# Forgetting attention: the keys' biases as rows of the product for the maxima, and the maxima's row made by products with the identity

## The chip, the cores and the metric

One core of a Trainium2 chip runs the whole program. The metric is the device time of one execution in microseconds (us). The median of three runs of the kernel before is 1830.58 us (1828.81 to 1836.41).

## What is computed

One layer of a streaming encoder: 2,048 prompt tokens and 8 x 16 sample tokens go through an RMS norm and one wide projection, whose columns feed three mixers: forgetting attention (6 heads of 64), RWKV-7 time mixing and cross-attention to 256 memory tokens (4 heads of 64). The gated results go through an output projection. The change touches the two attentions on the prompt. Cut to what matters:

```python
def fox_attend_block(q, cq, qpos, k, v, ck, kpos):
    s = jnp.einsum('bqhd,bkhd->bhqk', q, k) * (HEAD_DIM ** -0.5)
    s = s + jnp.transpose(cq, (0, 2, 1))[..., :, None] - jnp.transpose(ck, (0, 2, 1))[..., None, :]
    s = jnp.where(kpos[None, :] <= qpos[:, None], s, jnp.finfo(jnp.float32).min)
    p = jax.nn.softmax(s, axis=-1)
    return jnp.einsum('bhqk,bkhd->bqhd', p, v)
# c = cumsum(log forget) along the tokens; memory attention is the same without c and without the mask
```

## The kernel before

The program has two parts. The first (to about 1125 us) projects the tokens and runs RWKV-7; it writes queries, keys and values to DRAM (`q_d`, `k_d`, `v_d`). At its end `forget()` (L788) sums the log forget values and writes the keys' biases, -c, as six rows of 2,048 to `nc_d`. The second part does the attentions and the output projection.

In the second part the work of forgetting attention comes in 12 **units**, one for each pair of heads `hp` (0 to 2) and block `qb` (0 to 3) of 512 queries; "unit (1,3)" is pair 1, block 3. Block `qb` sees `qb + 1` blocks of 512 keys. Memory attention has 8 units more. Around them stand the sample tokens' attention (`sample`, L1188) and the output projection (`py`).

A unit has two steps. The first, `queries` (L1034), finds for every query the largest logit. `fox_max` multiplies 128 queries by 512 keys into `pm` on TensorE (PE), and VectorE (DVE) adds the keys' biases and takes the maximum in one instruction (L1063). The biases lie in `nb`, a tile of [128, 2, 2048] into which every row of `nc_d` is copied to all 128 partitions, 256 KB in each of 24 transfers (L1011). There is one `nb`, so the next pair's biases wait until the last maximum of this pair is done. `negate` turns the signs, and `rows_` turns the eight columns of maxima into a row: a transpose on PE (`pr`), a copy on ScalarE (ACT, `m8`), a transfer to DRAM (`md`), and two transfers back into partition 64 of `Q2` (L1086, L1088).

The second step, `attend` (L1100), forms keys x queries in `pS` from two products: `K1` x `Q1` (128 rows: the keys' upper part twice, against the queries' upper and lower parts) and `K2` x `Q2` (65 rows: the keys' lower part and a row of ones, against the queries' upper part and the row of negative maxima). So the second product can't start before that row has come back. ACT takes the exponential (L1117) and its rounded copy `Ph`, GpSimd (POOL) the remainder `Pl`, and three products per tile make `po`. Two `pS` buffers and two `pm` buffers are in use.

All transfers are issued by SyncE (SP), in one order. That order, and that of every engine, is set by a planner (`_arrange`, L1881) which takes the whole program's instructions, their costs and dependences by a model, tries 15 orders, and keeps one. So an edit in the second part can change the order everywhere, the first part included.

Of the kernel before, what the change touches and what calls it, by code (L numbers as in the profile page):

```python
# [33 lines left out]
TP = 2048  # L34
# [17 lines left out]
def kernel(ctx: ExitStack, tc: tile.TileContext, I: dict, O: dict):  # L52
# [8 lines left out]
    def tt(e, out, a, b, op):  # L61
        e.tensor_tensor(out=out, in0=a, in1=b, op=op)  # L62
# [52 lines left out]
    nc_d = dt("nc_d", [6, TP])  # L115
# [7 lines left out]
    with ExitStack() as p1:  # L123
# [664 lines left out]
        def forget():  # L788
# [137 lines left out]
    with ExitStack() as p2:  # L926
# [21 lines left out]
        S.copy(negT, negm[:, 2, :])  # L948
        idb = c2t("idb", [128, 128], BF16)
# [46 lines left out]
        def fox_keys(U, hp):  # L996
# [4 lines left out]
            def block(g0):  # L1001
                if not g0:
                    U["nb"] = kp.tile([128, 2, TP], F32, tag="nb", name="nb")
                gs = slice(g0, g0 + 512)
                pt = turned_in(k_d[gs, cs], 512)
                k1 = [kp.tile([128, 512], F32R, tag="K1", name="K1", bufs=2 * NKB) for _ in range(2)]
                k2 = [kp.tile([65, 512], F32R, tag="K2", name="K2", bufs=2 * NKB) for _ in range(2)]
# [11 lines left out]
        def mem_keys(U, hp):  # L1019
            cs = slice(128 * hp, 128 * hp + 128)  # L1020

            def step():
# [3 lines left out]
                k1 = [m[:, 256 * h:256 * h + 256] for h in range(2)]  # L1026
                k2 = [m[0:65, 512 + 256 * h:768 + 256 * h] for h in range(2)]
# [6 lines left out]
        def queries(U, q, qsrc, qb, hp, fox):  # L1034

            s_ = "" if fox else "m"

            def load():
                pt = turned_in(qsrc, 512)
                if fox:  # L1040
                    q["Q1"] = [wk.tile([128, 512], F32R, tag=f"Q1{h}", name=f"Q1{h}") for h in range(2)]
                    q["Q2"] = [wk.tile([65, 512], F32R, tag=f"Q2{h}", name=f"Q2{h}") for h in range(2)]
                else:
                    m = big("Qm", F32R)
                    q["Q1"] = [m[:, 512 * h:512 * h + 512] for h in range(2)]
                    q["Q2"] = [m[0:65, 512 * h:512 * h + 512] for h in (2, 3)]
# [965 lines left out]
```

## Time and profile before

| | |
|---|---|
| median of 3 runs | 1830.58 us |
| the profiled execution: its own time | 1832.25 us |
| its span in the profile | 1830.5 us |
| PE busy | 1718.1 us, 94% of the span |
| DVE, ACT, POOL busy | 51%, 48%, 43% |
| mean clock granted to PE | 0.971 |

The profiled execution is 1.67 us slower than the median of the runs; 1.75 us of it lie around the span. PE is the busiest engine, so time is won or lost where PE is idle, or where it is granted its lower clock; both are looked for by stretches of the span. A wait in brackets, as `[5.40 <-DVE Q L62]`, is idle time of that engine just before the instruction, with what ended it. SPq rows are the issues of transfers, not the transfers themselves.

### The profile page before, as it was taken

To read this page: it belongs to the slowest core of one execution; us is meant where nothing else is said; L and a number is where in the kernel's file an instruction comes from. 1 tells how busy PE (TensorE), PEld (TensorE's weight loads), DVE (VectorE), ACT (ScalarE), POOL (GpSimd) and SP (SyncE) were. 2 spreads that over 40 slices of the span, in tenths; PEclk is the share of its full clock that TensorE was granted. 3 is DMA by queue.
4 is the path that set the end of the run, shared out by engine and by line. 5 is a ranking of instruction groups with operands and counts; after the bars stand their busy time and mean duration, and the time that the engine had idled before them with its cause. 6 is when DMAs were issued, how large, how long until landed. Compare 5 with 4: busy or idle time off the path is not lost. (4 is left out here: it accounts for less than half of the span.)

```text
span 1830.5 us, 42049 instructions
## 1 busy us (share of the span) xinstructions
PE 1718.1 (94%) x16743; PEld 1370.1 (75%) x16743; DVE 934.0 (51%) x2325; ACT 872.3 (48%) x1727; POOL 782.4 (43%) x790
## 2 busy tenths in 40 slices
PE   4989999999999999999999998799899898999998
PEld 3989989788887788887888886567576555667776
DVE  6543354474444564364754543867346654485213
ACT  5424342533243424325232433687787565986351
POOL 5565252232322243031322241377586364866562
PEclk9999999999999999999999998799999898999999
DMA  7665463644445645456454454434647645262432
GB/s 230 246 219 200 144 205 125 202 163 151 168 157 168 223 128 190 138 174 195 155 170 134 134 177 123 156 121 143 203 138 248 195 141 173 87 209 87 163 111 89
DMA packets 213273, 301.34 MB, mean 165 GB/s; under 512 B 57444, under 2 KB 162454, under 8 KB 197206
## 3 DMA queue, kind: packets, MB, share of 16 engines
q1 hardware_dynamic: 213078, 298.66, 49.6%
q8 instruction: 131, 2.15, 0.5%
q14 instruction: 64, 0.52, 0.1%
HBM read 211.47 MB, written 87.12 MB: 163 GB/s over the span
## 5 line engine op out<-in xcount | busy, mean ns | idle before, releaser
L59 PE MATMUL pjd<-xk,w 128*128 128x512 f32 (+4 forms) x2280 | 520.1, 373 | 14.6 <-DVE xk L62 6.7
L59 PEld LDWEIGHTS pjd<-xk,w 128*128 128x128 f32 (+1 forms) x2280 | 381.9, 190 | 79.1 <-issue 10.8
L62 POOL TENSOR_TENSOR Pl<-P,Ph 128x512 fp32r<-128x512 f32 (+3 forms) x272 | 315.5, 1174 | 150.5 <-ACT Ph L1120 127.6
L59 PE MATMUL pjt<-w,xk 128*128 128x256 f32 x2040 | 292.6, 291 | 4.4 <-ACT qk L705 4.4
L59 PEld LDWEIGHTS pjt<-w,xk 128*128 128x128 f32 x2040 | 263.9, 191 | 17.9 <-issue 7.7
L59 PE MATMUL py<-W,oh 128*128 128x512 f32 x816 | 236.2, 402 | 2.3 <-DVE rb L1162 1.6
L1117 ACT ACTIVATE P<-pS,NB 128x512 f32<-128x512 f32 x240 | 147.9, 623 | 85.6 <-PE pS L59 57.5
L59 PEld LDWEIGHTS py<-W,oh 128*128 128x128 f32 x816 | 150.5, 190 | 38.3 <-DVE rb L1162 2.1
L59 PE MATMUL pS<-Q,K 128*128 128x512 f32 (+2 forms) x480 | 155.5, 392 | 8.3 <-ACT P L1117 8.0
L1120 ACT CAST Ph<-P 128x512 fp32r<-128x512 f32 (+3 forms) x272 | 150.1, 564 | 7.7 <-PE po L59 2.9
L59 PE MATMUL po<-Ph,vt 128*65 128x512 f32 x480 | 151.3, 373 | 1.2 <-ACT ob L1143 0.7
L59 PEld LDWEIGHTS pS<-Q,K 128*128 128x128 f32 (+1 forms) x480 | 87.4, 195 | 40.5 <-ACT P L1117 24.7
L62 DVE TENSOR_TENSOR xo<-py,xo 128x512 f32<-128x512 f32 x68 | 46.5, 686 | 133.1 <-PE py L59 127.8
L59 PE MATMUL pm<-K,Q 128*128 128x512 f32 (+2 forms) x240 | 95.8, 411 | 19.5 <-DVE Q L62 13.1
L62 POOL TENSOR_TENSOR nr<-nr,mhalf 128x8 f32<-128x8 f32 (+2 forms) x43 | 61.2, 1424 | 122.9 <-DVE nr L68 106.4
L1063 DVE CUSTOM_DVE_ANT_0 jk<-pm,nb,mx 128x512 bf16<-128x512 f32 (+3 forms) x144 | 93.2, 647 | 33.7 <-PE pm L59 25.1
L62 POOL TENSOR_TENSOR w<-wraw,w 128x1024 fp32r<-128x1024 f32 (+1 forms) x34 | 79.6, 2343 | 46.6 <-ACT w L197 42.2
L59 PE MATMUL po<-Pl,vt 128*65 128x512 f32 x240 | 88.3, 369 | 1.8 <-POOL Pl L62 1.7
L705 ACT COPY qk<-pjt 128x512 f32<-128x512 f32 (+1 forms) x47 | 26.5, 563 | 131.0 <-PE pjt L59 104.3
L59 PEld LDWEIGHTS po<-Ph,vt 128*65 128x65 f32 x480 | 64.0, 139 | 27.3 <-ACT Ph L1120 2.4
L59 PEld LDWEIGHTS pm<-K,Q 128*128 128x128 f32 x240 | 47.1, 198 | 44.7 <-DVE mx L1063 18.2
L62 POOL TENSOR_TENSOR oh<-ot,oh 128x384 fp32r<-128x384 f32 (+2 forms) x38 | 44.9, 1183 | 74.3 <-ACT oh L1323 39.5
(392 smaller groups left out, 2820.9 us busy)
## 6 DMA issues: line engine op xcount, KB each, us to landing
w<-w_d SPq DMA_DIRECT2D x84, 1024.0 KB
w_d<-w SPq DMA_DIRECT2D x28, 1024.0 KB
y_d<-xo SPq DMA_DIRECT2D x21, 512.0 KB
wraw<-in_w_in SPq DMA_DIRECT2D x36, 256.0 KB
xo<-in_x SPq DMA_DIRECT2D x17, 512.0 KB
xo<-y_d SPq DMA_DIRECT2D x17, 512.0 KB
xt<-in_x SPq DMA_DIRECT2D x24, 256.0 KB
xraw<-in_xT SPq DMA_DIRECT2D x24, 256.0 KB
```

What stands on the lines that cost most here:

```text
L59: PE.matmul(out, lhsT, rhs, start=start, stop=stop, skip_group_check=True)
L62: e.tensor_tensor(out=out, in0=a, in1=b, op=op)
L705: S.copy(o_, out)
L1063: V.tensor_tensor_reduce(out=jk[:, :n], in0=pm[:, :n], in1=U["nb"][:, h, c0:c0 + n], scale=1.0, scalar=-3.0e38 if c0 == 0 else m_, op0=A_, ...
L1117: S.activation(P_[:, c0:], pS[:, c0:], AF.Exp, bias=NB[:, qb, 2 * hp + h, kt:kt + 1] if fox else 0.0)
L1120: S.copy(Ph[:, c0:], P_[:, c0:])
```

## The change

- `forget` writes the biases as an upper and a lower part, so `nc_d` has 12 rows; the copy out of `pn` moves to ACT, with a subtraction on DVE.
- `nb` and its 24 transfers of 256 KB go. `K1` becomes [67, 512]: the keys' upper part, a row of ones, and the two rows of the bias, which 24 transfers of 4 KB bring from `nc_d`. `Q1` becomes [67, 512]: the queries' upper part and three rows of ones, the first of which is later overwritten by the negative maximum. `K2` and `Q2` become 128 rows, and hold the two cross products.
- `fox_max` multiplies 67 rows, and its maximum is a plain reduction out of PSUM into a column of its own; a small reduction joins the columns where `qb` is not 0.
- `negate` writes columns 0 and 32 of a tile `turnm`, the rest of which is zero. `rows_` makes four products of 33 columns with the identity, and two copies on ACT of [1, 512] from PSUM straight into `Q1`. The transfers by way of `md` go, 60 in all.
- In `attend` the product without the row of maxima now comes first.

```diff
-    nc_d = dt("nc_d", [6, TP])
+    nc_d = dt("nc_d", [12, TP])
...
-            nr = sm.tile([96, 128], F32, tag="w4", name="nr", bufs=1)
-            V.tensor_copy(nr, pn[0:96, 0:128])
-            SY.dma_start(nc_d.rearrange("h (t p) -> (h t) p", p=128), nr)
+            nr = sm.tile([96, 2, 128], F32R, tag="w4", name="nr", bufs=1)
+            S.copy(nr[:, 0], pn[0:96, 0:128])
+            tt(V, nr[:, 1], pn[0:96, 0:128], nr[:, 0].bitcast(F32), SUB)
+            for a in range(2):
+                SY.dma_start(nc_d[6 * a:6 * a + 6].rearrange("h (t p) -> (h t) p", p=128), nr[:, a].bitcast(F32))
...
+        turnm = [c2t(f"turnm{j}", [128, 4, 33], F32R) for j in range(4)]
+        for x in turnm:
+            G.memset(x.bitcast(F32), 0.0)
...
         def split_keys(k1, k2, src, n):
             src = src[:, :n]
             S.copy(k1[0:64, :n], src)
-            S.copy(k1[64:128, :n], src)
-            tt(V, k2[0:64, :n], src, k1[0:64, :n].bitcast(F32), SUB)
-            G.memset(k2[64:65, :n].bitcast(F32), 1.0)
+            S.copy(k2[0:64, :n], src)
+            tt(V, k2[64:128, :n], src, k1[0:64, :n].bitcast(F32), SUB)
+            G.memset(k1[64:65, :n].bitcast(F32), 1.0)
...
                 for h in range(2):
                     split_keys(k1[h], k2[h], pt[64 * h:64 * h + 64], 512)
-                for h in range(2):
-                    SY.dma_start(U["nb"][:, h, gs], nc_d[2 * hp + h, gs].partition_broadcast(128))
+                    SY.dma_start(k1[h][65:67, :].bitcast(F32), nc_d[2 * hp + h:2 * hp + h + 7:6, gs])
...
                     S.copy(q["Q1"][h][0:64], src)
-                    S.copy(q["Q2"][h][0:64], src)
-                    tt(V, q["Q1"][h][64:128], src, q["Q1"][h][0:64].bitcast(F32), SUB)
+                    S.copy(q["Q2"][h][64:128], src)
+                    tt(V, q["Q2"][h][0:64], src, q["Q1"][h][0:64].bitcast(F32), SUB)
+                    if fox:
+                        G.memset(q["Q1"][h][64:67].bitcast(F32), 1.0)
...
-                V.tensor_tensor_reduce(out=jk[:, :n], in0=pm[:, :n], in1=U["nb"][:, h, c0:c0 + n], scale=1.0,
-                                       scalar=-3.0e38 if c0 == 0 else m_, op0=A_, op1=MAX, accum_out=m_)
+                V.tensor_reduce(out=q["mx"][:, h, t, c0 // 512:c0 // 512 + 1], in_=pm[:, :n], op=MAX, axis=AX.X)
...
             def rows_():
                 pr = qa.tile([128, 512], F32, tag="pt", bufs=PTB, name="pr")
-                PE.transpose(pr[0:8, 0:128], q["mx"].rearrange("p h t -> p (h t)"), ident)
-                m8 = wk.tile([8, 128], F32R, tag="m8", name="m8")
-                S.copy(m8, pr[0:8, 0:128])
-                md = dt("md", [8, 128], bufs=4)
-                SY.dma_start(md, m8.bitcast(F32))
+                for t in range(4):
+                    mm(pr[0:33, 128 * t:128 * t + 128], q["mr"][:, t, :], idr)
                 for h in range(2):
-                    SY.dma_start(q["Q2"][h][64:65, :].bitcast(F32), md[4 * h:4 * h + 4].rearrange("(o t) c -> o (t c)", o=1))
+                    S.copy(q["Q1"][h][64:65], pr[32 * h:32 * h + 1])
...
-                mm(pS[:, c0:], k1, q["Q1"][h][:, c0:], stop=False)
+                mm(pS[:, c0:], k2, q["Q2"][h][:, c0:], stop=False)
                 diag = fox and kt >= 4 * qb
-                mm(pS[:, c0:], k2, q["Q2"][h][:, c0:], start=False, stop=not diag)
+                mm(pS[:, c0:], k1[0:65], q["Q1"][h][0:65, c0:], start=False, stop=not diag)
```

Counted over the whole program, PE gets 80 products of 33 columns for 20 transposes; DVE loses 240 reads of an accumulator, and 240 maxima become plain reductions; ACT gets 40 copies of [1, 512] for 20 of [8, 128]; POOL gets 24 memsets of [3, 512] and 4 of [128, 132]; SP issues 1,171 transfers for 1,230. In the first part only `forget` differs in its instructions, but the planner's order there is another from its first products on.

SP at the start of the second part, where the first keys, values and queries are loaded (`tok`, `vtok`); before:

```order
L980 DMA tok<-q_d 128x4x128
L941 DMA negm<-in_negm 128x384
L1011 DMA nb<-nc_d 128x512 x6
L754 DMA mg_d<-gth 128x512
L1011 DMA nb<-nc_d 128x512
L980 DMA tok<-k_d 128x4x128
L1011 DMA nb<-nc_d 128x512
L647 DMA o_d<-bv 128x512
L754 DMA mg_d<-gth 128x512
L923 DMA out_rs_p<-sstp 64x6x64
L988 DMA vtok<-v_d 128x4x128
L980 DMA tok<-q_d 128x4x128
```

and of the change:

```order
L990 DMA tok<-q_d 128x4x128
L943 DMA negm<-in_negm 128x384
L754 DMA mg_d<-gth 128x512 x2
L925 DMA out_rs_p<-sstp 64x6x64
L647 DMA o_d<-bv 128x512
L1018 DMA K_13992<-nc_d 2x512
L990 DMA tok<-k_d 128x4x128
L998 DMA vtok<-v_d 128x4x128
L990 DMA tok<-q_d 128x4x128
L1018 DMA K_13993<-nc_d 2x512
```

Eight loads of `nb` stood ahead of the second `vtok` and `tok<-q_d`; one load of bias rows stands there now, and the other head's follows.

SP around the end of pair 1, where the biases of pair 2 are fetched; before, with the row of maxima of unit (1,3) (`md<-m`, `Q<-md`) among them:

```order
L1011 DMA nb<-nc_d 128x512
L1086 DMA md<-m_18747 8x128
L980 DMA tok<-q_d 128x4x128
L1198 DMA sC<-mg_d 128x128
L1206 DMA sC<-mq_d 128x128
L1011 DMA nb<-nc_d 128x512 x6
L1170 DMA rc<-sd 32x32
L1088 DMA Q_18194<-md 1x512
L1088 DMA Q_18195<-md 1x512
```

and of the change:

```order
L990 DMA tok<-q_d 128x4x128
L1158 DMA sd<-rs 1x512
L1210 DMA sC<-mg_d 128x128
L1218 DMA sC<-mq_d 128x128
L1018 DMA K_18810<-nc_d 2x512
L1182 DMA rc<-sd 32x32
L1018 DMA K_18811<-nc_d 2x512
L1185 DMA rd<-rc 32x32
```

The row and the six loads ahead of its return are gone from the queue.

PE from the row of maxima of unit (1,3) to that unit's first product that needs it (before `Q_18194`, the change `Q_18091`); before:

```order
L1082 MATMUL pr<-ident,mx 8x128
L59 MATMUL pS_18734<-sB,sD 32x256 x4
L1263 MATMUL pt3b<-ident,sD 128x128 x2
L59 MATMUL pS_18810<-sB,sD 32x256 x4
L1263 MATMUL pt3b<-ident,sD 128x128 x2
L59 MATMUL po_18861<-sD,sA 64x16 x32
L1211 MATMUL pt_18964<-ident,sC 128x128
L59 MATMUL pS<-Q_18194,K_16179 128x512 x2
```

and of the change:

```order
L59 MATMUL pr<-idr,turnm_13967 33x128 x4
L59 LDWEIGHTS idb
L59 MATMUL pS<-negT,idb 128x128
L59 MATMUL po<-Ph,vt 65x512
L59 MATMUL po<-Ph,vt 64x512
L59 MATMUL po<-Pl,vt 65x512
L59 MATMUL po<-Ph,vt 65x384
L59 MATMUL pS<-Q_18091,K_16117 128x512
```

Between the two stood the small products of a sample's attention (`sB`, `sD`, `sA`); now a few products of the unit before stand there.

## Rows read from the trace of the kernel before

**Rows 1.** Profile page, head and the busy time of PE.
```profile
span 1830.5 us, 42049 instructions
PE 1718.1 (94%) x16743; PEld 1370.1 (75%) x16743; DVE 934.0 (51%) x2325; ACT 872.3 (48%) x1727; POOL 782.4 (43%) x790
```

**Rows 2.** Stretches of the span: length, busy time and instructions of each engine, granted clock of PE, busy share of the DMA engines, GB/s. The first row is the first part, the last the whole second part.
```profile
0.00:1125.00 1125.00, 1071.60 (x13220) 918.40 (x13221) 554.96 (x1445) 411.34 (x859) 374.99 (x408) 0.98 0.52 172
1125.00:1170.00 45.00, 28.65 (x124) 19.06 (x122) 30.45 (x72) 23.80 (x47) 11.68 (x17) 0.62 0.66 207
1170.00:1410.00 240.00, 230.97 (x1108) 162.03 (x1109) 144.57 (x312) 185.71 (x350) 165.72 (x152) 0.99 0.49 161
1410.00:1445.00 35.00, 28.15 (x248) 17.94 (x247) 21.41 (x68) 18.82 (x41) 9.26 (x14) 0.80 0.56 182
1530.00:1550.00 20.00, 13.25 (x109) 8.39 (x107) 6.04 (x23) 8.90 (x20) 3.93 (x6) 0.66 0.84 244
1125.00:1830.50 705.50, 646.53 (x3525) 451.70 (x3523) 378.99 (x880) 460.93 (x868) 407.43 (x383) 0.95 0.47 154
```

**Rows 3.** Waits of PE in the second part (1125 to 1830): us in total, times, longest.
```profile
PE pm L59 <- DVE Q L62: 13.1, 6, 5.4
PE pS L59 <- ACT P L1117: 10.9, 12, 2.9
PE pt3b L1263 <- DVE sD L68: 8.3, 6, 3.1
PE pm L59 <- DVE mx L1063: 6.5, 13, 1.0
PE po L59 <- POOL Pl L62: 2.0, 5, 0.7
```

**Rows 4.** Start of the second part in order of time: start, us, engine, line, operation.
```profile
1127.92 4.39 SPq L1011 DMA_DIRECT2D nb<-nc_d  x6
1139.51 0.52 SPq L980 DMA_DIRECT2D tok<-q_d  x1
1151.05 0.80 PE L59 MATMUL pm<-K,Q 128*128 128x512 f32 x1 [5.40 <-DVE Q L62]
1154.69 0.87 PE L59 MATMUL pm<-K,Q 128*128 128x512 f32 x2 [2.84 <-DVE Q L62]
```

**Rows 5.** One of the stretches in it, columns as in rows 2.
```profile
1135.00:1140.00 5.00, 3.48 (x11) 2.35 (x11) 3.06 (x10) 1.53 (x4) 0.00 (x0) 0.50 1.05 366
```

**Rows 6.** Unit (1,1), from its maxima's way to DRAM to their way back, in order of time.
```profile
1417.81 0.29 SPq L1086 DMA_DIRECT2D md<-m  x1
1424.73 3.66 SPq L1202 DMA_DIRECT2D sC<-np_d  x8
1429.15 1.30 PE L1263 MATMUL pt3b<-ident,sD 128*128 128x128 f32 x5 [3.08 <-DVE sD L68]
1430.41 0.57 SPq L1088 DMA_DIRECT2D Q<-md  x2
```

**Rows 7.** Unit (1,3), the same way, to the first product that reads the row.
```profile
1532.62 0.28 SPq L1086 DMA_DIRECT2D md<-m  x1
1534.70 4.35 SPq L1011 DMA_DIRECT2D nb<-nc_d  x6
1539.57 0.57 SPq L1088 DMA_DIRECT2D Q<-md  x2
1543.10 1.22 PE L59 MATMUL pS<-Q,K 65*128 65x512 f32 x2
```

**Rows 8.** Unit (0,3) in order of time, the same way; the last row is output projection that PE took meanwhile.
```profile
1289.25 0.28 SPq L1086 DMA_DIRECT2D md<-m  x1
1294.37 0.57 SPq L1088 DMA_DIRECT2D Q<-md  x2
1300.72 4.15 PE L59 MATMUL py<-W,oh 128*128 128x512 f32 x17
```

**Rows 9.** Two stretches behind it, columns as in rows 2.
```profile
1305.00:1310.00 5.00, 3.00 (x15) 1.67 (x14) 1.29 (x2) 2.88 (x5) 2.24 (x2) 1.00 0.68 229
1310.00:1315.00 5.00, 2.23 (x6) 1.11 (x7) 2.52 (x5) 4.23 (x9) 2.61 (x3) 0.86 0.94 274
```

**Rows 10.** Groups by form, whole span: busy us, mean ns of one, then idle before.
```profile
L1063 DVE CUSTOM_DVE_ANT_0 jk<-pm,nb,mx 128x512 bf16<-128x512 f32 x90 | 67.2, 747 | 22.9 <-PE pm L59 18.4
L1063 DVE CUSTOM_DVE_ANT_0 jk<-pm,nb 128x512 bf16<-128x512 f32 x78 | 53.6, 687 | 18.4 <-PE pm L59 14.5
L1063 DVE DVE_READ_ACCUMULATOR2_ANT mx<- 128x1 f32 x240 | 19.6, 82 | 0.0
L1070 DVE TENSOR_REDUCE mx<-pm 128x2 f32<-128x512 f32 x32 | 21.3, 686 | 7.3 <-PE pm L59 7.2
L59 PE MATMUL pS<-Q,K 128*128 128x512 f32 x168 | 73.3, 438 | 6.0 <-ACT P L1117 5.7
L59 PE MATMUL pS<-Q,K 65*128 65x512 f32 x168 | 68.3, 413 | 0.0
L1139 ACT COPY rs<-po 1x512 f32<-1x512 f32 x20 | 11.6, 580 | 18.3 <-PE po L59 18.0
L975 POOL MEMSET K<- 1x512 f32 x24 | 12.1, 520 | 1.0
```

**Rows 11.** The copy of the turned maxima: duration ns min/median/max, first and last start.
```profile
L1084 ACT CAST m<-pr x20: 238/255/256, 1144.3 to 1706.2; 8x128 fp32r<-8x128 f32 x20
```

**Rows 12.** A piece of the chain that ended last: start, us, what. Four transposes of 128 columns in a row.
```profile
1308.47 0.45 PE pt L983 x4
```

**Rows 13.** A wait of SP in the second part.
```profile
SPq L1011 <- DVE mx L68: 5.5, 2, 3.5
```

More of the change, by code (lines that the diff above doesn't have):

```diff
@@ L948 @@
         S.copy(negT, negm[:, 2, :])
+        idr = c2t("idr", [128, 128], F32R)
+        S.copy(idr, ident)
+        turnm = [c2t(f"turnm{j}", [128, 4, 33], F32R) for j in range(4)]
+        for x in turnm:
+            G.memset(x.bitcast(F32), 0.0)
+        taken = [0, 0]
         idb = c2t("idb", [128, 128], BF16)
@@ L1001, in block @@
             def block(g0):
[L1002 to L1003 removed]
                 gs = slice(g0, g0 + 512)
                 pt = turned_in(k_d[gs, cs], 512)
[L1006 to L1007 removed]
+                k1 = [kp.tile([67, 512], F32R, tag="K1", name="K1", bufs=2 * NKB) for _ in range(2)]
+                k2 = [kp.tile([128, 512], F32R, tag="K2", name="K2", bufs=2 * NKB) for _ in range(2)]
                 for h in range(2):
                     split_keys(k1[h], k2[h], pt[64 * h:64 * h + 64], 512)
[L1010 to L1011 removed]
+                    SY.dma_start(k1[h][65:67, :].bitcast(F32), nc_d[2 * hp + h:2 * hp + h + 7:6, gs])
                 vt = kp.tile([128, 1032], F32R, tag="vt", name="vt", bufs=NKB)
@@ L1025, in step @@
                 pt = turned_in(mk_d[:, cs], 256)
-                k1 = [m[:, 256 * h:256 * h + 256] for h in range(2)]
-                k2 = [m[0:65, 512 + 256 * h:768 + 256 * h] for h in range(2)]
+                k1 = [m[0:65, 256 * h:256 * h + 256] for h in range(2)]
+                k2 = [m[:, 512 + 256 * h:768 + 256 * h] for h in range(2)]
                 for h in range(2):
@@ L1040, in load @@
                 if fox:
-                    q["Q1"] = [wk.tile([128, 512], F32R, tag=f"Q1{h}", name=f"Q1{h}") for h in range(2)]
-                    q["Q2"] = [wk.tile([65, 512], F32R, tag=f"Q2{h}", name=f"Q2{h}") for h in range(2)]
+                    q["Q1"] = [wk.tile([67, 512], F32R, tag=f"Q1{h}", name=f"Q1{h}") for h in range(2)]
+                    q["Q2"] = [wk.tile([128, 512], F32R, tag=f"Q2{h}", name=f"Q2{h}") for h in range(2)]
                 else:
                     m = big("Qm", F32R)
-                    q["Q1"] = [m[:, 512 * h:512 * h + 512] for h in range(2)]
-                    q["Q2"] = [m[0:65, 512 * h:512 * h + 512] for h in (2, 3)]
+                    q["Q1"] = [m[0:65, 512 * h:512 * h + 512] for h in range(2)]
+                    q["Q2"] = [m[:, 512 * h:512 * h + 512] for h in (2, 3)]
                 for h in range(2):
@@ L1068, in mem_max @@
                 for j in range(2):
[L1069 to L1070 removed]
+                    mm(pm[:, 256 * j:256 * j + 256], q["Q1"][h][0:64, 128 * (t + j):128 * (t + j) + 128],
+                       U["K1"][0][h][0:64])
+                V.tensor_reduce(out=q["mx"][:, h, t:t + 2, 0], in_=pm.rearrange("p (t k) -> p t k", k=256), op=MAX,
                                 axis=AX.X)
             def negate():
[L1074 to L1078 removed]
+                mx = q["mx"][:, :, :, 0]
+                if fox and qb:
+                    mx = wk.tile([128, 2, 4], F32, tag="m1", name="m1")
+                    V.tensor_reduce(out=mx.rearrange("p h t -> p (h t)"),
+                                    in_=q["mx"].rearrange("p h t c -> p (h t) c"), op=MAX, axis=AX.X)
+                for h in range(2):
+                    if fox:
+                        ts(V, q["mr"][:, :, 32 * h], mx[:, h], off[:, 4 * qb, 2 * hp + h:2 * hp + h + 1], -1.0, A_, M)
+                    else:
+                        ts(V, q["mr"][:, :, 32 * h], mx[:, h], -1.0, None, M, ALU.bypass)
             def rows_():
                 pr = qa.tile([128, 512], F32, tag="pt", bufs=PTB, name="pr")
[L1082 to L1086 removed]
+                for t in range(4):
+                    mm(pr[0:33, 128 * t:128 * t + 128], q["mr"][:, t, :], idr)
                 for h in range(2):
[L1088 removed]
+                    S.copy(q["Q1"][h][64:65], pr[32 * h:32 * h + 1])
             r = [load]
```

13 lines of the change are left out of this document (3 added, 10 removed).

## The prediction

> **What bounds the kernel now.** I read the page's head first: PE is busy 94% of a span of 1830.5 us [rows 1]. So no other engine's work counts by itself; what counts is where PE has nothing to do, and where it is granted its lower level. The table by stretches says where. The first part has 53.4 us without PE work in 1125 (1125 - 1071.6), spread out. Of the second part three short stretches stand out [rows 2]: its start (1125 to 1170: 16.35 us idle, granted clock 0.62), 1410 to 1445 (6.85 us idle, 0.80) and 1530 to 1550 (6.75 us idle, 0.66). A mean of 0.62 between full speed (2.4 GHz) and half (1.2 GHz) is 34 us at half; 0.80 is 14 us, 0.66 is 13.6 us. If the idle time lies in the time at half, the slower products lose half of the rest: 8.9, 3.6 and 3.4 us. So 25, 10.4 and 10.2 us can be won there at most.
>
> Then I asked the issues of transfers in each stretch what stood before PE.
> - Start: six loads of `nb` take SP 4.39 us, two more follow, and the second `tok<-q_d` is issued only at 1139.51; PE then waits 5.40 and 2.84 us for the split of those queries [rows 4]. From 1135 to 1140 the DMA engines are full (share 1.05) [rows 5].
> - Unit (1,1): the row of maxima leaves at 1417.81 and is fetched back at 1430.41, behind a sample's eight loads (3.66 us). For these 12.6 us the unit's second products can't run, and PE idles 3.08 us in a sample's chain that has nothing beside it [rows 6].
> - Unit (1,3): the row leaves at 1532.62, six `nb` loads hold SP for 4.35 us, the return is issued at 1539.57, and the first product that reads it starts at 1543.10: 10.5 us [rows 7].
> - Unit (0,3): 5.1 us between the two; PE covers it with 17 products of the output projection, and is then out of work, 4.77 us idle from 1305 to 1315 [rows 8, 9].
>
> **The change, part by part.** The sum is made against the profiled execution, 1832.25 us, 1.67 above the median of the runs.
>
> 1. *Start.* Eight loads of 256 KB go (2.1 MB; 5.7 us at the 366 GB/s of rows 5), and some 5 us of SP's issue with them; in the new order one load of bias rows stands ahead of the second `tok<-q_d`. That brings the queries forward by 4 to 6 us, and PE's two waits on them are 8.2 us. I take **-6**: most of the waits, plus some time at half clock. Bounds 0 and -12 (the waits, and nearly half of the 8.9 us of the clock). What is late next is ACT's and DVE's splitting of keys and queries, which nothing shortens.
> 2. *Unit (1,1).* The row now takes four products (four transposes of 128 columns: 0.45 us [rows 12]) and two copies of [1, 512] (0.58 each [rows 10]), 1.6 us for 12.6. In the new order the unit's own products follow within the samples' chain. **-5**, half of what is lost there; bounds 0 and -10.4. The sample's chain itself stays.
> 3. *Unit (1,3).* Here the row is all that is waited for, and both causes go. **-7**; bounds 0 and -10.2.
> 4. *Unit (0,3).* With no gap to fill, the 17 products remain for 1305 to 1315: **-2**, bounds 0 and -4.8. The other units' rows come back under dense PE work: 0.
> 5. *Maxima on DVE.* The 168 maxima of 512 columns took 67.2 + 53.6 us and 168 x 82 ns for the accumulator, 134.6 us; as plain reductions of 686 ns they take 115.2 [rows 10]. That is 19 us less on an engine off the path; what PE waits for it is 6.5 us [rows 3]. **-2**, bounds 0 and -6.5. The added small reductions and sign changes come out of that gain.
> 6. *PE.* Same number of `pm` and `pS` products and columns. 20 x 3 more small ones, 0.11 us each by rows 12, are 6.7 us if PE is dense; some fall into idle time: **+5**, bounds +2 and +6.7. `pm` has 67 rows for 128. The row of 65 rows has 413 ns, that of 128 rows 438 [rows 10]; read as a price of rows, it would be worth 168 x 25 ns = 4.2 us. I take nothing: the longer one is the first of its pair and carries the 6.0 us of waiting. The Trainium skill ("TensorE: Matmul & The Clock Gate", section "LDWEIGHTS") says that a load of 32 rows takes as long as one of 128; by it the 4.2 us are nothing too, and by the row alone the sum would be 4.2 lower.
> 7. *ACT.* 40 copies of 0.58 for 20 of 0.255 [rows 10, 11]: +18.1 us beside 460.9 busy in 705.5 [rows 2]. PE waits 10.9 us for ACT in all [rows 3]; the copies stand before a unit's first exponentials, where ACT has little to do: **+2**, bounds 0 and +18.1.
> 8. *POOL.* 24 memsets of 0.52 us [rows 10], 12.5 us beside 407 of 705.5 [rows 2]; PE waits 2.0 us for POOL [rows 3]. 0, at most +2.
> 9. *Transfers elsewhere, and the first part.* SP issues 59 fewer, and nothing waits for the rest of `nb`: 0. In the first part the instructions are the same but for `forget`; the order differs and no row says which is better: 0, within 5 either way (a tenth of its idle 53.4 us).
>
> Sum: -6 - 5 - 7 - 2 - 2 + 5 + 2 = **-15 us**, 1817.2 for the profiled execution and **1815.6** for the median of the runs (1830.58 - 15). About 0.5% (9.2 us) is what a measurement of this kernel tells from no change: below 1821.4 is faster, above 1839.7 slower.
>
> **The rivals.**
> - *The stalls move.* The row was one of several late things. For this speaks that in rows 6 the idle time just before the transposes is put down to DVE's `sD`, the sample's own chain, and that at the start ACT's splits come one after another. Against it: in rows 7 only the row was missing. And the new bias rows are a transfer too: a block's first maximum now waits for a load of 4 KB that SP can issue only when the old `K1` tile is free, with the queue behind it; SP held `nb` that way for 5.5 us already [rows 13]. Then steps 1 and 3 give 3 and 4, steps 2, 4 and 5 nothing, and with +5 and +2 the time stays at **1830.6**.
> - *ACT becomes the bound: slower.* From 1170 to 1410 ACT is busy 185.7 of 240 us [rows 2]; with 12 of the 20 units there it gets +10.9, a share of 0.82. If each copy stood ahead of an exponential that PE waits for, all 18.1 us would come on the path; steps 1 and 3 keep their 13, step 6 its 5: +10.1, **1840.7**. It decides from the point at which ACT has no idle time around a unit's start; the mean of 0.77 and the 10.9 us that PE waits for ACT now speak against it.
> - *A transfer's fixed price is all that goes.* The Trainium skill ("DMA: Bandwidth & Descriptors", section "Anatomy of one DMA") gives about 2 us for a transfer whatever its size. As a mechanism of this kernel: the row saves its two hops alone, and SP's queue stands as long as before, since other loads move up. A hop is bounded by rows 7: from its issue to the product that reads it the return takes 3.5 us, so two are 7 us of the 10.5, and of 12.6. Step 2 then shrinks to half, 2.5, and step 3 to two thirds, 4.7, and the sum to -10.2: **1820.4**. By the Trainium skill's figure, as an estimate, two hops are 4 us and the sum would be some 3 us higher still.
>
> **How the numbers follow.** Chances: the forecast 0.50, the fixed price alone 0.12, the stalls move 0.23, ACT 0.15. Faster by over 0.5%: nearly all of the forecast (0.45), more than half of the fixed price (0.08) and a third of the moved stalls, where the first part's new order may help (0.09): 0.62. Slower by over 0.5%: most of the ACT case (0.12) and a little of the moved stalls (0.02): 0.14. The rest, 0.24, is no change. All upper ends together (-12, -10.4, -10.2, -4.8, -6.5, with +2 and 0) would be -42 and 1788.7; that all come at once is unlikely, and the range stops at three quarters of it, -31.5: **1799**. Upwards it takes in the moved stalls with +3.4 for the order: **1834**. About 0.2 is left out, most of it the ACT case.
>
> **What would show it.** Right: SP's loads of keys and queries at the start issued by 1135; the three stretches gone or short, with a granted clock near 1; a unit's first product with the row 2 to 3 us behind its `pr`; DVE about 20 us less busy, ACT 18 more. Wrong: if PE idles as long at the second part's start, or the samples' chains still stand alone and at half clock, the stalls have moved; if PE's waits for ACT grow from 10.9 us by ten or more, it is ACT; if SP waits long at the loads of bias rows, it is the queue. If the first part's end moves by more than 5 us, the planner's order, which I took as neutral, decides the result.

## The result, and the profile after

The changed kernel takes 1835.79 us (median of 20 runs, 1830.02 to 1841.74), the kernel before 1831.34 beside it (20 runs): a ratio of 1.0027, 95% interval 1.0016 to 1.0037. It is slower by 0.27%, beyond the interval, but by the prediction's bound of 0.5% that is no change; it lies 20 us above the forecast and 1.8 us above the upper end of the range (1834). The head of its profile (5.1 us longer than [rows 1], with 26.6 us more PE work and 12.2 less on DVE):

```profile
span 1835.6 us, 41777 instructions
PE 1744.7 (95%) x16803; PEld 1389.7 (76%) x16803; DVE 921.8 (50%) x2102; ACT 888.8 (48%) x1749; POOL 793.3 (43%) x818
```

I divide both spans at the first transpose of the second part (`pt`, L983, now L993): 1129.68 us before, 1145.79 after. View: stretches, columns as in [rows 2]; the first 27 us, which are loads, are left out. Before:

```profile
27.00:1129.68 1102.68, 1067.99 (x13218) 915.37 (x13219) 547.49 (x1421) 401.31 (x838) 368.50 (x391) 0.98 0.52 170
1129.68:1830.50 700.82, 644.08 (x3503) 450.01 (x3502) 375.88 (x873) 459.66 (x865) 402.81 (x376) 0.95 0.47 154
```

After:

```profile
27.00:1145.79 1118.79, 1079.31 (x13222) 927.11 (x13220) 549.26 (x1418) 402.78 (x843) 369.91 (x397) 0.97 0.51 167
1145.79:1835.60 689.81, 658.38 (x3563) 458.24 (x3562) 363.11 (x650) 476.02 (x885) 414.66 (x401) 0.95 0.44 147
```

The second part became 11.0 us shorter: 25.3 us less without PE work (31.4 for 56.7), 14.3 us more PE work, with PE at half clock (1.2 GHz) for 73 us in both. The first part, in which the change touches two instructions and a DMA of `forget`, became 16.1 us longer, and 11.3 of these are PE *work*: the same products took longer.

Where it lies can be seen at the twelve RWKV chains (`gw`, `gx`: products of 32 by 32 that wait in turn for DVE and ACT). The order puts projection products (`pjd`) between their links to keep PE busy. View: timeline of one chain, before and after (start, us, engine, line, operation, idle time before it and its cause). Before:

```profile
830.71 0.75 PE L59 MATMUL gw<-x,gm 32*32 32x32 f32 x64
831.39 0.96 PE L59 MATMUL pjd<-xk,w 128*128 128x512 f32 x3
832.29 0.75 PE L59 MATMUL gw<-xd,g 32*32 32x32 f32 x64
832.97 1.90 PE L59 MATMUL pjd<-xk,w 128*128 128x512 f32 x7
834.79 0.69 PE L59 MATMUL gx<-x,gm 32*32 32x32 f32 x32
```

After:

```profile
851.27 0.75 PE L59 MATMUL gw<-x,gm 32*32 32x32 f32 x64 [0.66 <-DVE x L464]
852.49 1.05 PE L59 MATMUL gw<-xd,g 32*32 32x32 f32 x64 [0.47 <-ACT g L470]
853.47 0.45 PE L59 MATMUL pjd<-xk,w 128*70 128x512 f32 x1
855.59 1.06 PE L59 MATMUL gx<-x,gm 32*32 32x32 f32 x32 [1.67 <-DVE x L477]
```

Ten `pjd` stand between these links before, one after. The idle time of the twelve chains, each with the wait before its first link, added up from the timeline, is 7.8 us before and 17.3 after (elsewhere in the first part it falls, so that 4.8 us remain in all). It costs more than itself, since the granted clock falls behind it (stretches of the profile after):

```profile
850.00:855.00 5.00, 2.79 (x134) 2.08 (x132) 2.68 (x5) 1.91 (x5) 1.27 (x1) 0.94 0.93 311
855.00:860.00 5.00, 4.41 (x70) 2.96 (x70) 1.86 (x4) 3.39 (x8) 1.51 (x2) 0.50 0.97 340
860.00:865.00 5.00, 4.76 (x83) 3.09 (x82) 0.00 (x0) 2.34 (x5) 0.18 (x1) 0.50 0.48 157
865.00:870.00 5.00, 5.00 (x93) 4.09 (x92) 3.07 (x9) 1.11 (x4) 0.00 (x0) 0.50 0.51 200
```

Behind 2.21 us of idle time the products run at half clock (0.50) for 15 us and more. Added up over the first part, PE has half clock for 34 us before and 68 us after. The difference lies at the chains: of these times 13.7 and 47.8 us begin between the first and the last link of a chain, and 20.8 and 20.5 us elsewhere. Three chains after have only 4 to 7 projection products (`pjd`, `pjt`) between their links, where before none has fewer than 12; 30.7 of the 47.8 us begin in these three.

In the second part the waits that answer to [rows 3] (from 1145 us on: us in total, times, longest):

```profile
PE pm L59 <- DVE mx L1073: 5.0, 9, 1.2
PE pS L59 <- ACT P L1129: 4.7, 6, 2.1
PE pS L59 <- DVE Q L62: 2.6, 1, 2.6
PE pt3b L1275 <- DVE sD L68: 2.2, 2, 1.9
PE po L59 <- POOL Pl L62: 1.7, 3, 0.9
```

The longest one of before, `pm` for DVE's half of the queries (13.1 us), is gone, and those for `P` and `sD` are about half and a quarter.

### The profile page after: what moved, and what is told of

The parts are those of the page before. It is cut to its first block, busy times and chain, and to the rows that moved or that the text cites. A ratio compares the mean times of both kernels' runs of the same rounds, so it can differ in the third digit from the quotient of the medians.

```text
span 1835.6 us, 41777 instructions
## 1 busy us (share of the span) xinstructions
PE 1744.7 (95%) x16803; PEld 1389.7 (76%) x16803; DVE 921.8 (50%) x2102; ACT 888.8 (48%) x1749; POOL 793.3 (43%) x818
## 4 chain that ended last, share of the span: by engine, by line
PE 76%; DVE 5%; ACT 5%; DMA 4%; issue 4%; POOL 3%; SPq 1%; DVEq 0%; POOLq 0%; ACTq 0%
PE pjd L59 20%; PE pjt L59 11%; PE po L59 9%; PE py L59 9%; PE pS L59 6%; PE pm L59 4%; PE sc L59 2%; PE sy L59 2%; PE gr L59 1%; PE pa L59 1%; PE pz L59 1%; PE spr L59 1%; PE pbt L59 1%; PE pvt L59 1%; PE gw L59 1%
## 5 line engine op out<-in xcount | busy, mean ns | idle before, releaser
L59 PE MATMUL pjd<-xk,w 128*128 128x512 f32 (+4 forms) x2280 | 527.0, 378 | 12.1 <-ACT xk L270 7.1
L59 PEld LDWEIGHTS pjd<-xk,w 128*128 128x128 f32 (+1 forms) x2280 | 387.5, 192 | 80.7 <-issue 12.7
L59 PE MATMUL pjt<-w,xk 128*128 128x256 f32 x2040 | 284.3, 290 | 7.0 <-ACT qk L705 4.4
L59 PEld LDWEIGHTS pjt<-w,xk 128*128 128x128 f32 x2040 | 259.7, 192 | 16.8 <-issue 7.0
L59 PE MATMUL py<-W,oh 128*128 128x512 f32 x816 | 231.2, 401 | 1.5 <-DVE xo L62 1.2
L1073 DVE TENSOR_REDUCE mx<-pm 128x1 f32<-128x512 f32 (+2 forms) x240 | 139.9, 606 | 60.6 <-PE pm L59 58.5
L59 PE MATMUL pS<-Q,K 128*128 128x512 f32 (+1 forms) x480 | 154.6, 396 | 7.8 <-ACT P L1129 4.7
L62 DVE TENSOR_TENSOR xo<-py,xo 128x512 f32<-128x512 f32 x68 | 46.7, 689 | 142.5 <-PE py L59 134.2
L59 PEld LDWEIGHTS pS<-Q,K 128*128 128x128 f32 (+1 forms) x480 | 87.3, 197 | 38.7 <-ACT P L1129 18.2
L59 PE MATMUL pm<-K,Q 67*128 67x512 f32 (+2 forms) x240 | 95.6, 418 | 6.5 <-DVE mx L1073 5.0
L59 PEld LDWEIGHTS pm<-K,Q 67*128 67x128 f32 x240 | 49.7, 208 | 25.0 <-DVE mx L1073 12.1
```

The source lines that it names most:

```text
L59: PE.matmul(out, lhsT, rhs, start=start, stop=stop, skip_group_check=True)
L1073: V.tensor_reduce(out=q["mx"][:, h, t, c0 // 512:c0 // 512 + 1], in_=pm[:, :n], op=MAX, axis=AX.X)
```

## The experiments

All pairs of numbers for a part are split at the first `pt`, except in the first four expectations, which count from the first load of keys (`tok<-k_d`; 704.6 us before, 693.0 after).

### 1. Which part's order

The planner's result is replaced for the first part by a table of start times (`_FIRST`); the rest moves along.

```diff
     _, start = min(found, key=lambda x: x[0])
+    first = list(itertools.accumulate(array.array("i", zlib.decompress(base64.b85decode(_FIRST)))))
+    last = [max(t for x, t in enumerate(s[:len(first)]) if p.of[x] == "PE") for s in (first, start)]
+    start = first + [t + last[0] - last[1] for t in start[len(first):]]
```

**The change, first part as before.** Expected: 

> The changed kernel, with the start of every instruction of the first part (projections and RWKV) taken from the order of the kernel before, written into the kernel as a table; the second part keeps the order that the changed kernel has. Theory 'the order': the changed kernel lost 16.7 us in the first part (the first load of keys for the second part was issued at 1142.6 us, before at 1125.9) only because the planner picked another order there, and gained 11.6 us in the second (693.0 against 704.6 us from that load to the end). Then the load is at 1126 +- 2 us, the second part takes 693 +- 3 us, the time is 1820 +- 3 us, ratio to the kernel before 0.992 to 0.995. Rival 'forget': the two instructions and the DMA that the change adds to the first part delay it by themselves; then the load stays near 1142 and the time near 1836. Rival 'the seam': the slower first part had only hidden the loads of the second; then the load is at 1126, but the second part takes about 705 us and the time is 1831.

**The kernel before, first part as in the change.** Expected: 

> The kernel before, with the starts of the first part taken from the order that the changed kernel has; the second part keeps its own order. Theory 'the order': the first load of keys is issued at 1142.6 +- 2 us, the second part takes 704.6 +- 3 us, the time is 1848 +- 3 us, ratio 1.007 to 1.011. Rival 'forget' (the change's own instructions in the first part delay it): 1831, since they are not in this kernel. Rival 'the seam': load at 1142.6, the second part about 693, time 1836.

Measured: 1815.38 us, ratio 0.9923 [0.9898, 0.9948], load at 1124.3; and 1848.54 us, ratio 1.0097 [1.0072, 1.0122], load at 1144.0. The two, columns as above:

```profile
27.00:1127.78 1100.78, 1067.05 (x13218) 915.57 (x13219) 547.34 (x1420) 401.61 (x840) 368.19 (x393) 0.99 0.52 170
1127.78:1815.90 688.12, 657.27 (x3564) 456.64 (x3562) 363.33 (x650) 475.53 (x885) 414.19 (x402) 0.95 0.44 147
```

```profile
27.00:1147.17 1120.17, 1080.85 (x13221) 928.77 (x13220) 549.01 (x1418) 401.88 (x841) 368.84 (x394) 0.97 0.51 167
1147.17:1847.30 700.13, 646.86 (x3504) 452.50 (x3502) 371.90 (x873) 459.42 (x865) 401.95 (x376) 0.94 0.46 154
```

The first part follows its order and the second part its own, crosswise, within 2 us; only the time of the first run lies outside what was expected, 1.6 us below 1817 to 1823. `forget` and the seam are out. By the medians the new order of the first part costs 20.4 us in the change (1835.79 against 1815.38) and 18.2 us in the kernel before (1848.54 against 1830.33 beside it). The idle time in the chains goes with the order as well (7.1 and 17.2 us), and so does the half clock (31 and 75 us, of which 6.8 and 51.2 begin in a chain).

### 2. One part of the change alone

Both have the first part in the order of before; the planner orders the second part anew. The first restores the way over DRAM, the second the addition on VectorE (and the broadcast loads of `nb`):

```diff
-                for t in range(4):
-                    mm(pr[0:33, 128 * t:128 * t + 128], q["mr"][:, t, :], idr)
-                for h in range(2):
-                    S.copy(q["Q1"][h][64:65], pr[32 * h:32 * h + 1])
+                PE.transpose(pr[0:8, 0:128], q["mn"].rearrange("p h t -> p (h t)"), ident)
+                m8 = wk.tile([8, 128], F32R, tag="m8", name="m8")
+                S.copy(m8, pr[0:8, 0:128])
+                md = dt("md", [8, 128], bufs=4)
+                SY.dma_start(md, m8.bitcast(F32))
+                for h in range(2):
+                    SY.dma_start(q["Q1"][h][64:65, :].bitcast(F32), md[4 * h:4 * h + 4].rearrange("(o t) c -> o (t c)", o=1))
```

```diff
-                V.tensor_reduce(out=q["mx"][:, h, t, c0 // 512:c0 // 512 + 1], in_=pm[:, :n], op=MAX, axis=AX.X)
+                V.tensor_tensor_reduce(out=jk[:, :n], in0=pm[:, :n], in1=U["nb"][:, h, c0:c0 + n], scale=1.0,
+                                       scalar=-3.0e38 if c0 == 0 else m_, op0=A_, op1=MAX, accum_out=m_)
```

**Biases alone.** Expected: 

> The changed kernel with the biases as rows of the product, but the row of maxima over DRAM as before (transpose, copy of 8x128, one DMA out, two back into the row); the first part in the order of the kernel before. By the prediction's steps it keeps the start (-6 us) and the maxima (-2 us) and about +3 us of PE, and loses the steps on units (1,1), (1,3) and (0,3) (-14 us): the second part takes 700 us and the time is about 1826, ratio 0.997. Rival 'the rows are all': the second part stays at 704 to 706 us, time 1831. Rival 'the biases are all': 693 us, time 1820.

**Rows alone.** Expected: 

> The kernel before with the row of maxima by products with the identity, the biases still added on VectorE from broadcast loads; the first part in the order of the kernel before. By the prediction's steps it keeps the units (1,1), (1,3) and (0,3) (-14 us), less about 4 us for PE and ScalarE: the second part takes 694 to 697 us and the time is about 1822, ratio 0.995. Rival 'the rows are all': the second part is at 693 us, time 1820. Rival 'the biases are all': 704 to 706 us, time 1831.

Measured: biases alone 1830.64 us, ratio 0.9995 [0.9976, 1.0015], second part 703.8; rows alone 1812.66, ratio 0.9898 [0.9874, 0.9922], second part 686.1 (700.8 before). Counted from the first load of keys, as in the expectations, they are 707.0 and 689.8. It looked as if the rows were all, and more than the prediction gave them. The next runs took that back.

### 3. Every instruction at its old place

To see what the removed waits are worth without the planner, a table gives every instruction of both parts its place of before: the four products stand where the transpose stood, the two copies where the copy of 8x128 stood; what is gone leaves no gap.

```diff
-    found = []
...
-    _, start = min(found, key=lambda x: x[0])
+    start = list(itertools.accumulate(array.array("i", zlib.decompress(base64.b85decode(_STARTS)))))
```

**Rows.** Expected: 

> The row of maxima by products with the identity, biases still on VectorE (as in the run 'rows alone'), but with every instruction of both parts at the place that it has in the order of the kernel before: four products stand where the transpose stood, two copies where the copy of 8x128 stood, and the three DMAs are gone. From the first transpose of the second part (pt) to the end the kernel before takes 700.8 us, rows alone in its own order 686.1. Theory 'the waits': the gain is that of the prediction's steps on the units (1,1), (1,3) and (0,3), -14 us, less about 5 us for the products and copies: 690 to 694 us, time about 1822, ratio 0.994 to 0.997. Rival 'the re-planning': the gain of rows alone came from the planner, which could put the products of the scores earlier; then 698 to 702 us remain, time about 1830. Rival 'more than the waits': 686 us as in its own order, time 1813 to 1817.

**Biases.** Expected: 

> The biases as rows of the product and the plain reduction on VectorE, the row of maxima over DRAM, every instruction at the place that it has in the order of the kernel before (the load of a key block's two bias rows stands behind that block's split). Theory 'the waits': the start gains 6 us and the maxima 2 us, PE loses 1 to 3 us: from the first pt to the end 693 to 697 us against 700.8, time about 1826, ratio 0.996 to 0.998. Rival 'the biases bring nothing' (as in biases alone, where waits went but the granted clock fell): 700 to 704 us, time 1831 to 1835. The two are told apart by the start too: PE idle over 15 us in the first 40 us behind the seam goes to under 9 by the first, stays at 14 by the second.

**The change.** Expected: 

> The whole change, every instruction at the place that it has in the order of the kernel before. Theory 'the waits': the prediction's sum without the planner, -15 us: from the first pt to the end 684 to 689 us, time about 1816, ratio 0.990 to 0.994. Rival 'the re-planning': the waits go, but other instructions stand where they stood for the old latencies; 693 to 698 us, time 1824 to 1829. Rival 'the order decides all': 700 us, 1830.

| at the old places | time | ratio | second part | PE idle | PE busy |
|---|---|---|---|---|---|
| before | 1831.34 | | 700.8 | 56.7 | 644.1 |
| rows | 1841.99 | 1.0068 [1.0047, 1.0089] | 714.0 | 59.5 | 654.5 |
| biases | 1850.28 | 1.0114 [1.0097, 1.0132] | 721.5 | 51.7 | 669.8 |
| the change | 1860.63 | 1.0164 [1.0140, 1.0189] | 729.6 | 53.6 | 676.0 |

All three are slower than the kernel before, outside every expectation, and in their second parts PE stands at half clock for 86, 113 and 120 us (in this order) for 73 before. For the rows, unit (1,3) shows why (timeline of PE and its waits; to be held against [rows 7], where the row of maxima came back over DRAM):

```profile
1537.18 0.43 PE L59 MATMUL pr<-idr,turnm 128*33 128x128 f32 x4 [0.85 <-DVE turnm L68]
1537.54 0.64 PE L59 MATMUL pS<-sB,sD 128*32 128x256 f32 x8
1540.24 0.49 PE L1269 MATMUL pt3b<-ident,sD 128*128 128x128 f32 x2 [2.06 <-DVE sD L68]
1540.66 1.08 PE L59 MATMUL pS<-sB,sD 128*32 128x256 f32 x8
1543.80 0.66 PE L1269 MATMUL pt3b<-ident,sD 128*128 128x128 f32 x2 [2.06 <-DVE sD L68]
1544.92 3.60 PE L59 MATMUL po<-sD,sA 128*64 128x16 f32 x64 [0.46 <-ACT sD L1270]
1548.95 0.47 PE L1217 MATMUL pt<-ident,sC 128*128 128x128 f32 x1 [0.42 <-DVE sC L65]
1549.07 1.20 PE L59 MATMUL pS<-Q,K 65*128 65x512 f32 x2
```

From `pr` to the first product that reads the row 11.9 us pass, as they did before (11.3: 1531.76 to [rows 7]'s 1543.10), though no transfer is left. The same stretch before (three lines of the timeline of PE):

```profile
1531.76 0.27 PE L1082 MATMUL pr<-ident,mx 128*8 128x128 f32 x1 [0.84 <-DVE mx L68]
1534.66 0.41 PE L1263 MATMUL pt3b<-ident,sD 128*128 128x128 f32 x2 [2.06 <-DVE sD L68]
1537.70 0.66 PE L1263 MATMUL pt3b<-ident,sD 128*128 128x128 f32 x2 [2.04 <-DVE sD L68]
```

PE has the same order in both: a sample's chain stands in between, and that chain waits for DVE's `sD`. The row was never what PE waited for: in the whole profile of before no wait of PE is put down to a load of it. That the planner had put the chain there because its model has the row late is likely, but not shown. Over the second part idle time even went up by 2.8 us, and PE work by 10.4, of which the products of `pr` can be only a part, since there is more half clock too.

For the biases, two waits of PE in the second part stand where `pm` had waited 13.1 us for DVE's half of the queries (waits of PE from 1126 us on):

```profile
PE pm L59 <- ACT Q L1050: 5.7, 2, 3.0
PE pm L59 <- DMA K<-nc_d: 3.9, 2, 3.7
```

The second is a load of bias rows that comes late. The rival "the stalls move" had named it; in the change's own order it is not there.

### 4. 67 rows or 128

The biases at the old places have 5 us less idle time than the kernel before and 25.7 us more PE work, at a mean granted clock of 0.92 in the second part for 0.95. What differs in PE's large products is that `pm` fills 67 rows for 128. This run gives it 128 again:

```diff
-                k1 = [kp.tile([67, 512], F32R, tag="K1", name="K1", bufs=2 * NKB) for _ in range(2)]
+                k1 = [kp.tile([128, 512], F32R, tag="K1", name="K1", bufs=2 * NKB) for _ in range(2)]
-            G.memset(k1[64:65, :n].bitcast(F32), 1.0)
+            G.memset(k1[64:, :n].bitcast(F32), 1.0)
-                        G.memset(q["Q1"][h][64:67].bitcast(F32), 1.0)
+                        G.memset(q["Q1"][h][64:128].bitcast(F32), 1.0)
```

Expected: 

> The run 'biases in the old order' with its products for the maxima over 128 rows instead of 67: the rows 67 to 127 of both operands hold ones (the two memsets reach down to row 127), which adds a constant that falls out again in the normalisation. Same instructions, same order. With 67 rows that run took 721.5 us from the first pt to the end, PE busy 669.8 us, at half the clock for 123 us; the kernel before 700.8, 644.1 and 74. Theory 'the rows and the clock': TensorE was granted full clock less often because its products filled 67 rows instead of 128; with 128 rows it is at half clock for 70 to 90 us, PE is busy 645 to 655 us, the second part takes 700 to 708 us, the time is 1830 to 1837. Rival 'the clock followed the waits': it stays at 115 to 125 us, 719 to 724 us, time 1849.

Measured: 1843.87 us, ratio 1.0059 [1.0028, 1.0090]. The 40 to 80 us behind the seam, where the two have hardly drifted apart, with 67 rows and then with 128 (columns as in [rows 2]):

```profile
1166.39:1206.39 40.00, 37.81 (x164) 25.29 (x165) 28.90 (x53) 28.61 (x57) 23.35 (x24) 0.91 0.41 125
```

```profile
1167.48:1207.48 40.00, 37.27 (x178) 25.10 (x178) 30.93 (x55) 30.25 (x61) 25.50 (x26) 1.00 0.42 128
```

With 67 rows PE has less idle time, and yet the lower clock, and gets 164 products done for 178. Over the second part half clock falls from 113 to 59 us (the 123 and 74 us of the expectation are read too high; the granted clock gives 113 and 73), and the length from 721.5 to 705.3, as the theory had it. But that execution (1835.57) is one of the fastest of ten (1831.03 to 1853.79), and their median meets neither the theory's 1830 to 1837 nor the rival's 1849. By the medians 6.6 of the 18.9 us above the kernel before come back and 12.3 remain, and the granted clock of the executions rises from 0.963 to 0.9685 (the kernel before has 0.971). So the filled rows are part of it, about a third; where the rest lies is open.

### 5. The same tries of the planner

The planner keeps one of fifteen tries, by the sum of both parts. Here the second part's try is set by hand, the first part is in the order of before. The 4000 ns in the second diff are to keep the parts apart at the seam; rows alone at these tries has them too, the change has not. The first load of keys is issued 3 to 4 us before the first `pt` in all of these runs.

```diff
-    _, start = min(found, key=lambda x: x[0])
+    _, start = found[2]
```

In the kernel before:

```diff
+    n, other = 8357, found[2][1]
+    last = [max(t for x, t in enumerate(s[:n]) if p.of[x] == "PE") for s in (start, other)]
+    start = start[:n] + [t + last[0] - last[1] + 4000 for t in other[n:]]
```

**Before, twelfth try:** 

> The kernel before with no instruction changed: the first part in its own order, the second part in the order of another of the planner's fifteen tries (weight 0.6, second round). Theory 'the order matters in the second part as well': the second part is more than 5 us off 700.8 us, shorter or longer, without any change to the work; time below 1826 or above 1836. Rival 'the second part is bound by its work': 699 to 703 us, time 1829 to 1833.

**The change, twelfth and thirteenth:** 

> The whole change, first part in the order of the kernel before, second part in the order of the planner's twelfth try (weight 0.6, second round) instead of its fifteenth; the kernel before took 709.0 us from the first pt to the end in the order of that try, the change in its own order 688.1. Theory 'the change shortens what the planner has to work round': the second part is 8 us or more below the 709.0 of the kernel before at the same try, 685 to 700 us. Rival 'the gain was the luck of one try': it is 700 to 712 us.

> As the run before, with the thirteenth try (weight 0.6, third round), the one that the planner kept for the kernel before (700.8 us in the second part). Theory 'the change shortens what the planner has to work round': 683 to 693 us. Rival 'the luck of one try': 697 to 708 us.

**Rows alone, thirteenth:** 

> Rows alone (row of maxima by products with the identity, biases on VectorE), first part in the order of the kernel before, second part in the order of the planner's thirteenth try; in its own order rows alone took 686.1 us, the kernel before at this try 700.8. Theory 'the rows carry the gain': 684 to 692 us. Rival 'the luck of one try': 697 to 708 us.

**Third try, before and change:** 

> The kernel before, its own order in the first part, the order of the planner's third try (weight 0.3, third round) in the second. So far its second part took 700.8 us (thirteenth try) and 709.0 (twelfth), from the first pt to the end. Theory 'the change gives the planner room': the kernel before stays between 698 and 712 us at every try. Rival 'the draw': it reaches 685 to 697 us at some tries as well.

> The whole change, first part in the order of the kernel before, second part in the order of the planner's third try. So far 688.1 us (fifteenth), 693.6 (twelfth), 706.4 (thirteenth). Theory 'the change gives the planner room': 685 to 698 us, and at least 6 us under the kernel before at this try. Rival 'the draw': anywhere from 688 to 710 us, with no fixed side to the kernel before.

**Fifth try, before and change:** 

> The kernel before, its own order in the first part, the order of the planner's fifth try (weight 0.3, fifth round) in the second. Theory 'the change gives the planner room': 698 to 712 us from the first pt to the end. Rival 'the draw': it may be 685 to 697 us.

> The whole change, first part in the order of the kernel before, second part in the order of the planner's fifth try. Theory 'the change gives the planner room': 685 to 698 us, and at least 6 us under the kernel before at this try. Rival 'the draw': anywhere from 688 to 710 us, on either side of the kernel before.

**Rows alone, third and fifth:** 

> Rows alone (row of maxima by products with the identity, biases on VectorE as before), first part in the order of the kernel before, second part in the order of the planner's third try. There the kernel before took 697.5 us from the first pt to the end, biases alone 703.8, the change 684.2. Theory 'the rows carry the gain': 681 to 689 us. Rival 'only both together': 693 to 700 us.

> Rows alone, second part in the order of the planner's fifth try, where the kernel before took 706.8 us from the first pt to the end and the change 691.4. Theory 'the rows carry the gain': 686 to 695 us. Rival 'only both together': 700 to 708 us.

Second part in us, from one profile each (PE idle in brackets; "own" is the try that the planner keeps for that kernel); 700.1 and 689.8 in second profiles of the first and last column's own tries:

| try | before | rows alone | biases alone | the change |
|---|---|---|---|---|
| 3 | 697.5 (46.7) | 694.9 (39.9) | 703.8 (34.0), own | 684.2 (26.0) |
| 5 | 706.8 (54.0) | 704.4 (45.0) | | 691.4 (31.7) |
| 12 | 709.0 (56.4) | | | 693.6 (33.8) |
| 13 | 700.8 (56.7), own | 701.9 (47.0) | | 706.4 (34.8) |
| 2 | | 686.1 (36.0), own | | |
| 15 | | | | 688.1 (30.8), own |

The draw is worth 11 us for the kernel before, 18 for rows alone, 22 for the change. At the same try the change is 13.3, 15.4 and 15.4 us shorter and once 5.6 longer: 9.6 on average, with one of four against the theory (the thirteenth, at a granted clock of 0.93 for 0.95); by four pairs with such a scatter the size of that gain is not settled. The theory's other half, that the kernel before stays above 698 us at every try, fails by half a microsecond at the third. The kernel before in the twelfth try was run 12 times: 1836.14 us, ratio 1.0024 [1.0009, 1.0039].

Rows alone are 2.6 and 2.4 shorter and 1.1 longer: nothing, by this scatter. So rows alone owed its 686.1 to a good try, and at the third and the fifth its times are those that "only both together" gave; biases alone was run at one of them only. What holds at every try is the exchange: the change has 21 to 23 us less idle time, and pays with about 7 us more PE work at three tries and 27.5 at the thirteenth, where PE stands at half clock for 102 us instead of 73. Both halves have a share in it. At the third try, where all four stand, rows alone have 6.8 us less idle time than the kernel before, biases alone 12.7, both together 20.7; but biases alone stand at half clock for 108 us, the other three for 77 to 87, and their PE work is 19 us more than that of the kernel before, which is more than they gain.

Fastest of all were rows alone in its own order (1812.66 us), the change in the third try (1813.78, one run) and the change with the old first part (1815.38). The first and the last beat the kernel before by more than 0.5% and beyond their intervals; whether the three differ among themselves these runs don't show.

## Why the prediction was wrong

- **Step 9 failed**, "the order differs and no row says which is better: 0, within 5 either way". It was +16.1 us in the profiles of before and after, 18 to 20 by the medians of section 1; over the eighteen profiles with the old order of the first part and the two with the new, the seam lies at 1127.0 and 1146.5 on average. The text's last condition (first part's end moved by more than 5 us) is what happened, but it was given neither a price nor a chance. The bound was taken from the idle time alone, a tenth of 53.4 us; of the 16.1 us 4.8 are idle time, and 11.3 are PE work, which took longer at half clock. A sign of it could have been had beforehand: how many projection products stand between the links of each chain can be counted in the two orders.
- The rest of the sum came out, -15 forecast, and 1815.38 us for 1830.33 measured with the first part held; but not for its reasons, and so by luck: at other tries of the planner the second part of the change is 13 to 15 us shorter or 6 longer than that of the kernel before at the same try (section 5), and in the old places steps 1 to 8 come to +28.8 us.
- *Step 1* (-6) right in size: the second `tok<-q_d` is issued 4.5 us behind the seam (1150.33) for 9.8 ([rows 4], 1139.51), and PE has 35.82 us of work in the 45 us that answer to [rows 2]'s 28.65. A part of it was not seen: `pm` now reads ACT's copy of the queries alone and not DVE's rest, and the wait of 13.1 us for that is gone. It needs the new order too: with the biases at the old places the first 40 us have 14.1 us of idle time, as before, since the waits for ACT's copy and for the bias rows take its place (section 3).
- *Steps 2 to 4* (-14) wrong. They priced how late the row was, not what PE waited for: [rows 6] names `sD`, not `md`, as what ended PE's wait, and the rival "the stalls move" said so; in [rows 7] the product that reads the row shows no wait at all, so "all that is waited for" (step 3) was not to be read there. Rows alone give 1.3 us on average at common tries.
- *Step 5* right in the price, 686 ns for a plain reduction of 512 columns (168 of them keep DVE busy for 111.8 us, forecast 115.2; DVE has 12.2 us less work in all, about 20 forecast), and nearly so on PE's path: its waits for `mx` fell from 6.5 to 5.0 us (forecast -2).
- *Step 6* (+5, at most +6.7) too small: +14.3 us of PE work in the second part, at the same half clock, and in no single group (the largest: `pr` 8.8 us for 5.5, the memory units' `pm`, now of 64 rows, 16.5 for 13.4, and `pt` 33.5 for 30.5). Taking nothing for the 67 rows was right for the time of the products, which at full clock is the same for 67 and for 128 rows (last section); what the rows cost in clock at the old places (section 4) was not seen. The rule that the step cites is on weight loads. The Trainium skill ("TensorE: Matmul & The Clock Gate", section "LDWEIGHTS (loading the stationary operand)") counts columns, not rows, for a weight load; the trace agrees, 208 ns on average for a load of 67 rows (after) and 198 for one of 128 (before) in `pm`.
- *Step 7* right in the work, 16.5 us more on ACT (forecast 18.1); the +2 on PE's path is not seen, PE's wait for `P` fell from 10.9 to 4.7 us. ACT did not become the bound. *Step 8* right: PE waits 1.7 us for POOL, 2.0 before.
- No rival had a time near 1835.8 by a cause that held. The stalls did move at the old places, but with 11 to 29 us on top that it did not have. The section of the Trainium skill that the third rival cites gives its 2 us for transfers that GpSimd issues; the row's were issued by SyncE, and the trace has no landing times for them.

## What to carry to other kernels

Where a planner orders a program, an edit changes the order of parts that it does not touch, and that can cost as much as the edit brings: hold the other part's order when you measure, and compare several orders before you credit an edit (one order each would here have credited rows alone with 14.7 us in the second part, where three common tries give 1.3). Ask of a late operand what PE's next instruction really waits for; if other work stands in front of its reader, taking the delay away gives nothing in that order. Price an idle gap with the half clock behind it, not by its own length.

## What the runs showed of the hardware

- One and the same order of the first part ended between 1119.66 and 1135.44 us in eighteen profiles, with 15 to 34 us at half clock. The mean granted clock of an execution goes with its time: in 17 runs of the kernel before it lay between 0.967 and 0.980, and 0.001 of it went with about 1.1 us.
- Products that fill 67 of 128 rows took no less time (`pm` of 512 columns at full clock: 412 ns, with 128 rows 413, in the two runs of section 4), and went with a lower granted clock at the same order and less idle time.
- A product of 64 rows on 256 columns (the memory units' `pm`) took 333 ns on average after, with 128 rows 293 before, all 64 of them at full clock in both; why is not shown.
